# Moving a feed-forward's first norm into the output projection's loop, with half-token block products and first activations put ahead

## The chip, the cores and the metric

The kernel runs on one core of a Trainium2 chip. The metric is the device time of one execution in microseconds (us); of several runs the median is compared. TensorE multiplies matrices into PSUM, VectorE and ScalarE work element by element and can read PSUM, GpSimd works element by element in SBUF, and DMA transfers are issued from the queues of SyncE (loads) and ScalarE (stores).

## The reference, cut to what matters

Two layers run one after the other over 1024 tokens of width 1024. The first mixes tokens by windowed attention and a gated delta rule, projects the mix and applies a feed-forward. The change touches only this last part of the first layer:

```python
def _rmsnorm(x, w):
    ...
    y = x32 * lax.rsqrt(jnp.mean(x32 * x32, axis=-1, keepdims=True) + EPS)
    return (y * w.astype(jnp.float32)).astype(x.dtype)

def first_block(...):
    ...
        h = h + jnp.concatenate([attn, gdn], axis=-1) @ w_out[l]
        hn = _rmsnorm(h, norm_ffn_w[l])
        h = h + jnp.square(jax.nn.relu(hn @ w_ffn_in[l])) @ w_ffn_out[l]
    return _rmsnorm(h, norm_final_w)
```

w_out is 1024 x 1024, w_ffn_in 1024 x 4096 and w_ffn_out 4096 x 1024, all float32. The second layer follows and is not touched.

## The kernel before, in words

All large products are made in three matmuls each (`mm3`, `accumulate`): an operand is kept as a rounded part H and the rest L, and H·H, H·L and L·H are summed in PSUM. H is made by a cast on ScalarE; L by a subtraction on VectorE or GpSimd. `weight` (lines 103 to 113) loads a weight tile into one of three "raw" slots and splits it into one of eight "wh" and "wl" slots each.

The program says what is computed from what, in an order of text; the framework under it lays the tiles of the pools out in SBUF, orders the instructions of each engine by a plan made when the program is built, and makes a tile wait for the last use of what lay in its place before. So an engine's order need not be that of the text, but on the chip each engine and queue then keeps the order of the plan.

*Output projection.* First the attention half is projected, by column half n and token chunk i (128 tokens), into `Hs[i, n]`, 16 tiles of the pool "h" (lines 744 to 757). Then eight weight tiles are held in all the weight slots, and the loop of lines 762 to 787 goes over the eight chunks in the order 3, 4, 2, 5, 1, 6, 0, 7: ScalarE, GpSimd and VectorE prepare the gated and normed delta-rule output of the chunk (eight ScalarE operations), and TensorE multiplies it, 12 matmuls for each column half, which are added to `Hs` on VectorE (line 787).

*Norm of the feed-forward.* After the loop its pools and the PSUM pools are closed and new ones opened (lines 788 to 810). The loop of lines 829 to 861 goes over the chunks in the same order, p = 0 to 7: the sums of squares (line 164) and the root give a scale; `h` is stored to DRAM as the residual (line 835); VectorE scales (line 837); TensorE transposes eight blocks of 128 x 128 into two PSUM tiles (line 840). For the first four chunks ScalarE copies them as B00, B10, in float32 and as H, and VectorE makes L (lines 846, 826, 827). For the last four, VectorE forms the sums of a Strassen-like scheme against the first four, t1 to t4, and all are split into B11, T1, T2, T3, T4 (lines 851 to 861). A pair of such tiles takes 16 KB of each partition; the pool "xs" has 14 tiles of 8 KB, and "tx" six of 2 KB beside the norm's weights (4 KB).

*First product.* `strassen` (lines 904 to 933) makes 256 of the 4096 hidden rows in one of 16 groups: seven block products of 12 matmuls with 512 tokens each, where a plain product has eight. Two of them, A00 with B00 and A01 with B10, need only the first 512 tokens; the others need T2, T1, T3, T4 and B11, with weight sums S1 to S4 made on VectorE (lines 915, 916, 922, 930) from weights loaded to the pool "f1" (line 886; 44 KB, of which four weight tiles are 16, six sums 12, and eight tiles for results 16). Each group is a generator in two parts; lines 935 to 941 put the first part of group g + 2 behind the second part of group g. `hidden` (lines 897 to 902) adds, applies relu and square on VectorE, and stores to `hid_d` in DRAM.

*Second product.* Lines 963 to 983: for c = 0 to 7 four weight tiles of each column half are loaded and split, then 512 hidden rows are loaded (line 969) and split into D; at c = 0 the residual is loaded from `h_d` into the new tiles `Hs` (line 976); then 16 sums of 12 matmuls are added to `Hs` on VectorE (line 981).

Of the kernel before, what the change touches and what calls it, by code (L numbers as in the profile page):

```python
# [17 lines left out]
P = 128  # L18
# [38 lines left out]
def tile_hybrid_layers(ctx, tc, a, out):  # L57
# [464 lines left out]

    s2 = ctx.enter_context(ExitStack())
# [4 lines left out]
    op = pool(s2, "o", 8)  # L528
# [136 lines left out]

    project(*PA)
# [69 lines left out]
    s3.close()  # L736
    hpc = ctx.enter_context(ExitStack())
# [24 lines left out]
    for c in order:  # L762
# [20 lines left out]
        for n in range(2):  # L783
            ps = acc512()
            for k in range(4):
                mm3(ps, u, g[n][k], k == 0, k == 3, asl=hs(k))
            dve.tensor_add(Hs[c, n], Hs[c, n], ps)
    s4.close()
    s2.close()
# [8 lines left out]
    pm[0] = pool(pf, "pff", 6, space=PSUM)  # L798
    ptc = ctx.enter_context(ExitStack())
    pt = pool(ptc, "ptr", 2, space=PSUM)  # L800
    h_d, hid_d = scratch("h_d", [T, 1024]), scratch("hid_d", [4096, T])
# [4 lines left out]
    xsp = pool(s5, "xs", 14)  # L806
    txc = ctx.enter_context(ExitStack())
    txp = pool(txc, "tx", 6)
    wb = txp.tile([P, 1024], F32, name="wb", tag="wb", bufs=1)
    dma(wb, a["norm_ffn_w"][0].partition_broadcast(P))  # L810

    def xtile(name, dt=F32R):
        return xsp.tile([P, 4, 512], dt, name=name, tag="xs")

    def pair(name):
        return xtile(name + "h"), xtile(name + "l")

    def tx():
        return txp.tile([P, 4, P], F32, name="tx", tag="tx")


    B00f, B10f = xtile("x00", F32), xtile("x10", F32)
    B00, B10, B11, T2, T1, T3, T4 = (None,) * 7

    def halved(U, cs, src, eng):
        act.copy(U[0][:, :, cs], src)
        eng.tensor_sub(U[1][:, :, cs], src, f32(U[0][:, :, cs]))

    for p, i in enumerate(order):
        hv = [Hs[i, 0], Hs[i, 1]]  # L830
        cs = slice((p % 4) * P, (p % 4) * P + P)
        rs = rstd_of(hv)
        pq = []
        for j in range(2):
            put(h_d[i * P : (i + 1) * P, 512 * j : 512 * j + 512], hv[j])
            xs = tmp()
            dve.scalar_tensor_tensor(xs, hv[j], rs, wb[:, 512 * j : 512 * j + 512], op0=ALU.mult, op1=ALU.mult)
            ps = pt.tile([P, 512], F32, name="g", tag="g")
            for q in range(4):
                pe.transpose(ps[:, q * P : q * P + P], xs[:, q * P : q * P + P], ident)  # L840
            pq.append(ps.rearrange("p (k t) -> p k t", k=4))
        if p < 4:
            if p == 0:
                B00, B10 = pair("b00"), pair("b10")
            for U, Uf, src in ((B00, B00f, pq[0]), (B10, B10f, pq[1])):
                act.copy(Uf[:, :, cs], src)
                halved(U, cs, src, dve)
            continue
        if p == 4:
            B11, T2, T1, T3, T4 = (pair(n) for n in ("b11", "t2", "t1", "t3", "t4"))  # L850
        b11, t1, t2, t3, t4 = (tx() for _ in range(5))
        act.copy(b11, pq[1])
        dve.tensor_sub(t1, pq[0], B00f[:, :, cs])
        dve.tensor_sub(t3, b11, pq[0])
        halved(B11, cs, pq[1], dve)
        dve.tensor_sub(t2, b11, t1)
        halved(T2, cs, t2, gp)
        dve.tensor_sub(t4, B10f[:, :, cs], t2)
        halved(T1, cs, t1, dve)
        halved(T3, cs, t3, gp)  # L860
        halved(T4, cs, t4, dve)
    txc.close()
    hpc.close()

    f1 = ctx.enter_context(ExitStack())
# [543 lines left out]
```

## Time and profile before

| | |
|---|---|
| median of 3 runs | 2537.58 us (2537.42 to 2539.28) |
| the profiled execution's own time | 2540.82 us |
| its span, first to last instruction | 2538.7 us |
| mean granted TensorE clock | 0.971 |
| TensorE busy | 2353.8 us (93%), 10906 matmuls and transposes |
| VectorE, ScalarE, GpSimd busy | 1495.1, 1063.6, 982.7 us |
| moved by DMA | 310.43 MB |

Times in the rows count from the span's first instruction. A row of the timeline gives the start, the time taken, the engine, the line, the operation and its tiles; in square brackets stands the idle time of the engine before it and what ended it. Matmuls are pipelined, so the distance from start to start, not the time of one, says how fast they follow each other. PE is TensorE, DVE is VectorE, ACT ScalarE, POOL GpSimd and SP SyncE; a q behind the name is the engine's queue.

### The profile page before, as it was taken

How to read it: one execution, taken by the hardware profiler on the slowest of the kernel's cores; microseconds unless marked ns; L12 is line 12 of the kernel's file. 1: busy time of each engine (PE TensorE's matmuls, PEld its weight loads, DVE VectorE, ACT ScalarE, POOL GpSimd, SP SyncE). 2: the span in 40 equal slices, each digit the busy share in tenths (PEclk: the TensorE clock that was granted, in tenths of full speed). 3: DMA queues.
4: the chain of work that ended last, by engine and by line, in shares of the span. 5: the costliest groups of instructions: out<-in, count | busy, mean ns of one | idle time of the engine just before them, and what ended most of it. 6: DMA issues, size and time to landing. Idle time of an engine off the chain costs nothing. (4 is left out here: it accounts for less than half of the span.)

```text
span 2538.7 us, 31786 instructions
## 1 busy us (share of the span) xinstructions
PE 2353.8 (93%) x10906; PEld 1927.9 (76%) x10906; DVE 1495.1 (59%) x2726; ACT 1063.6 (42%) x2177; POOL 982.7 (39%) x822
## 2 busy tenths in 40 slices
PE   7898798989949999899999999989999999999998
PEld 5676578878738888788888788767777787888887
DVE  5779935776576555444344703989988885312113
ACT  5554214665542333222122522666555575233331
POOL 3346734433432122222223413445444443344353
PEclk9999999989969999999999999999999999999999
DMA  5785598655413333443232333222222225312123
GB/s 166 222 274 161 146 299 237 173 153 182 143 57 118 108 111 105 151 156 100 92 100 88 117 101 116 63 73 71 67 67 67 67 79 164 123 47 87 47 74 120
DMA packets 326228, 310.43 MB, mean 122 GB/s; under 512 B 46407, under 2 KB 243971, under 8 KB 326067
## 3 DMA queue, kind: packets, MB, share of 16 engines
q1 hardware_dynamic: 271827, 234.38, 31.5%
q10 hardware_dynamic: 54240, 74.03, 8.3%
q8 instruction: 86, 1.41, 0.2%
q14 instruction: 75, 0.61, 0.1%
HBM read 224.89 MB, written 85.54 MB: 122 GB/s over the span
## 5 line engine op out<-in xcount | busy, mean ns | idle before, releaser
L99 POOL TENSOR_TENSOR wl<-raw,wh 128x512 fp32r<-128x512 f32 x212 | 292.2, 1389 | 537.5 <-ACT wh L98 523.6
L147 PE MATMUL mm<-uh,wh 128*128 128x512 f32 x960 | 379.4, 395 | 0.2 <-DVE mx L1202 0.2
L149 PE MATMUL mm<-uh,wl 128*128 128x512 f32 x960 | 378.1, 394 | 0.0
L148 PE MATMUL mm<-ul,wh 128*128 128x512 f32 x960 | 377.7, 393 | 0.0
L98 ACT CAST wh<-raw 128x512 fp32r<-128x512 f32 (+1 forms) x213 | 129.4, 616 | 288.0 <-PE mm L149 105.7
L149 PEld LDWEIGHTS mm<-uh,wl 128*128 128x128 f32 x960 | 181.7, 189 | 39.5
L148 PEld LDWEIGHTS mm<-ul,wh 128*128 128x128 f32 x960 | 181.9, 189 | 35.5
L147 PEld LDWEIGHTS mm<-uh,wh 128*128 128x128 f32 x960 | 182.1, 190 | 34.9 <-DVE mx L1202 0.6
L147 PE MATMUL mm<-wh,hid 128*128 128x512 f32 x512 | 200.9, 393 | 8.0 <-ACT hid L98 8.0
L148 PE MATMUL mm<-wl,hid 128*128 128x512 f32 x512 | 200.3, 392 | 0.0
L149 PE MATMUL mm<-wh,hid 128*128 128x512 f32 x512 | 198.3, 389 | 0.0
L981 DVE TENSOR_TENSOR h<-h,mm 128x512 f32<-128x512 f32 x128 | 87.6, 686 | 174.1 <-PE mm L149 173.9
L147 PE MATMUL mm<-xnh,wh 128*128 128x512 f32 x352 | 145.5, 413 | 14.4 <-ACT t L300 6.6
L1151 POOL TENSOR_TENSOR ul<-u,uh 128x512 fp32r<-128x512 f32 (+3 forms) x96 | 105.6, 1101 | 134.7 <-DVE uh L1150 112.4
L110 POOL TENSOR_TENSOR wl<-raw,wh 128x512 fp32r<-128x512 f32 x72 | 101.9, 1415 | 121.2 <-DVE wh L109 46.5
L149 PE MATMUL mm<-xnh,wl 128*128 128x512 f32 x352 | 143.7, 408 | 0.0
L148 PE MATMUL mm<-xnl,wh 128*128 128x512 f32 x352 | 143.6, 408 | 0.0
L147 PEld LDWEIGHTS mm<-wh,hid 128*128 128x128 f32 x512 | 96.9, 189 | 28.8 <-ACT hid L98 8.4
L148 PEld LDWEIGHTS mm<-wl,hid 128*128 128x128 f32 x512 | 97.0, 189 | 20.1
L149 PEld LDWEIGHTS mm<-wh,hid 128*128 128x128 f32 x512 | 96.3, 188 | 20.0
L157 DVE TENSOR_SCALAR s<-s 128x512 f32<-128x512 f32 x32 | 26.3, 821 | 135.4 <-ACT s L156 135.4
L290 DVE SCALAR_TENSOR_TENSOR tc<-cv,cw,tc 128x512 f32<-128x512 f32 x96 | 98.2, 1023 | 4.8 <-ACT cv L278 2.9
(405 smaller groups left out, 5763.1 us busy)
## 6 DMA issues: line engine op xcount, KB each, us to landing
raw<-in_w_in SPq DMA_DIRECT2D x172, 256.0 KB
raw<-in_w_ffn_out SPq DMA_DIRECT2D x64, 256.0 KB
raw<-in_w_ffn_in SPq DMA_DIRECT2D x32, 512.0 KB
hid_d<-ht ACTq DMA_DIRECT2D x64, 256.0 KB
hr<-hid_d SPq DMA_DIRECT2D x32, 512.0 KB
e<-e_d SPq DMA_DIRECT2D x16, 512.0 KB
raw<-in_w_out SPq DMA_DIRECT2D x32, 256.0 KB
kv<-kv_d SPq DMA_DIRECT2D x16, 512.0 KB
```

What stands on the lines that cost most here:

```text
L98: act.copy(H, src)
L99: (eng or dve).tensor_sub(L, src, f32(H))
L110: gp.tensor_sub(L, raw, f32(H))
L147: pe.matmul(ps, A[0][:, asl], B[0][:, bsl], start=first, stop=False)
L148: pe.matmul(ps, A[0][:, asl], B[1][:, bsl], start=False, stop=False)
L149: pe.matmul(ps, A[1][:, asl], B[0][:, bsl], start=False, stop=last)
L157: dve.tensor_scalar(s, s, 1e18, 1.0, op0=ALU.min, op1=ALU.add)
L290: dve.scalar_tensor_tensor(acc, cv[:, o + t : o + t + 512], cw[:, t, c : c + 1], acc, op0=ALU.mult, op1=ALU.add)
L981: dve.tensor_add(Hs[order[p], n], Hs[order[p], n], ps)
L1151: gp.tensor_sub(uL[:, cs], u[:, cs], f32(uH[:, cs]))
```

## The change

The norm's work for a chunk becomes a function, `ffn_norm(p, banks)`, called inside the projection's loop two chunks late (for p - 2 after chunk p), for p = 6 behind the loop and for p = 7 between the first two of three half products. The tiles B00 and B10 lie in a new pool "xsa" opened before the loop; the transposed tiles of the last four chunks are copied to spare tiles of the pool "h" (`later`), and B11, T1, T2, T3 are built from them after the half products, in a pool "xsb"; T4 takes two tiles of "xsa" that are free by then. `half` makes a group's two products for the first 512 tokens; for the first three groups (`EARLY`) it is called ahead, with weights loaded through the "raw" slots. The generators are gone: each group follows whole. In the second product the hidden rows stand before the weights in the text, the first sums are copied into `Hs` on ScalarE, and the residual is loaded in quarters at c = 2 to 5 and added on GpSimd. The pool "o" is placed below those of the scan, which are closed earlier. The PSUM pool of the first product has eight tiles in place of six and two.

```diff
+    s2o = ctx.enter_context(ExitStack())
+    op = pool(s2o, "o", 8)
     s2 = ctx.enter_context(ExitStack())
...
-    op = pool(s2, "o", 8)
...
+
+    s2.close()
 
     project(*PA)
     project(*PZ)
...
     s3.close()
+    xac = ctx.enter_context(ExitStack())
+    xsa = pool(xac, "xsa", 6, side="right")
     hpc = ctx.enter_context(ExitStack())
     hp = pool(hpc, "h", 16, side="right")
...
 
     g = [[rows(WO, 4 + k, 512 * n) for k in range(4)] for n in range(2)]
     order = [3, 4, 2, 5, 1, 6, 0, 7]
-    for c in order:
+
+
+
+    h_d, hid_d = scratch("h_d", [T, 1024]), scratch("hid_d", [4096, T])
+    wb = xsa.tile([P, 1024], F32, name="wb", tag="wb", bufs=1)
+    dma(wb, a["norm_ffn_w"][0].partition_broadcast(P))
+
+    def xtile(name, dt=F32R, pl=xsa):
+        return pl.tile([P, 4, 512], dt, name=name, tag="xs")
+
+    def pair(name, pl=xsa):
+        return xtile(name + "h", F32R, pl), xtile(name + "l", F32R, pl)
+
+    def spare(name):
+
+        return hp.tile([P, 512], F32, name=name, tag="h")
+
+    def tx():
+        return spare("tx").rearrange("p (k t) -> p k t", k=4)
+
+    def halved(U, cs, src, eng):
+        act.copy(U[0][:, :, cs], src)
+        eng.tensor_sub(U[1][:, :, cs], src, f32(U[0][:, :, cs]))
+
+    B00f, B10f = xtile("x00", F32), xtile("x10", F32)
+    B00, B10 = pair("b00"), pair("b10")
+    later = {}
+
+    def ffn_norm(p, banks):
+        i = order[p]
+        hv = [Hs[i, 0], Hs[i, 1]]
+        cs = slice((p % 4) * P, (p % 4) * P + P)
+        rs = rstd_of(hv)
+        for j, ps in enumerate(banks):
+            put(h_d[i * P : (i + 1) * P, 512 * j : 512 * j + 512], hv[j])
+            xs = tmp()
+            dve.scalar_tensor_tensor(xs, hv[j], rs, wb[:, 512 * j : 512 * j + 512], op0=ALU.mult, op1=ALU.mult)
+            for q in range(4):
+                pe.transpose(ps[:, q * P : q * P + P], xs[:, q * P : q * P + P], ident)
+            src = ps.rearrange("p (k t) -> p k t", k=4)
+            if p < 4:
+                act.copy((B00f, B10f)[j][:, :, cs], src)
+                halved((B00, B10)[j], cs, src, dve)
+            else:
+                later[p, j] = tx()
+                act.copy(later[p, j], src)
+
+    for p, c in enumerate(order):
         o = OC[c]
         qT = gu.tile([P, 512], F32, name="l1", tag="l1")
         dma(qT.rearrange("p (h c) -> p h c", h=4), gq_d[:, :, c * P : (c + 1) * P].rearrange("h p c -> p h c"))
@@ -785,8 +837,11 @@
             for k in range(4):
                 mm3(ps, u, g[n][k], k == 0, k == 3, asl=hs(k))
             dve.tensor_add(Hs[c, n], Hs[c, n], ps)
+        if p > 1:
+            ffn_norm(p - 2, (bank(), bank2()))
+    ffn_norm(6, (bank(), bank2()))
     s4.close()
-    s2.close()
+    s2o.close()
     rb.close()
     pb.close()
     pmc.close()
...
     pf = ctx.enter_context(ExitStack())
-    pm[0] = pool(pf, "pff", 6, space=PSUM)
-    ptc = ctx.enter_context(ExitStack())
-    pt = pool(ptc, "ptr", 2, space=PSUM)
-    h_d, hid_d = scratch("h_d", [T, 1024]), scratch("hid_d", [4096, T])
+    pm[0] = pool(pf, "pff", 8, space=PSUM)
     x2_d = scratch("x2_d", [T, 1024])
     sv_d = scratch("sv_d", [T, 512])
     W2 = a["w_in_2"][0]
     s5 = ctx.enter_context(ExitStack())
-    xsp = pool(s5, "xs", 14)
...
-    for p, i in enumerate(order):
...
-    txc.close()
-    hpc.close()
-
-    f1 = ctx.enter_context(ExitStack())
-    fp = pool(f1, "f1", 4, side="right")
+    xsb = pool(s5, "xsb", 8)
...
+
+    first, EARLY = [], 3
+
+    def half(c0, A00, A01, mu, ht):
+
+        pa, pb_ = acc512(), acc512()
+        accumulate(pa, operand(A00, gp), B00, True)
+        m1 = mu("m1")
+        act.copy(m1, pa)
+        accumulate(pb_, operand(A01, gp), B10, True)
+        hidden(pb_, m1, c0, 0, ht)
+        return pa
+
+    def hidden(ps, other, row, h, ht):
+
+        t = ht("ht")
+        dve.tensor_add(t, other, ps)
+        dve.scalar_tensor_tensor(t, t, 0.0, t, op0=ALU.max, op1=ALU.mult)
+        put(hid_d[row : row + P, 512 * h : 512 * h + 512], t)
+
+    for g in range(EARLY):
+        A = []
+        for j in range(2):
+            raw = wp.tile([P, 512], F32, name="raw", tag="raw", bufs=3).rearrange("p (k m) -> p k m", k=4)
+            dma(raw, F1[512 * j : 512 * j + 512, 256 * g : 256 * g + P].rearrange("(k p) m -> p k m", p=P))
+            A.append(raw)
+        first.append(half(256 * g, *A, spare, spare))
+        if g == 0:
+            ffn_norm(7, (acc512(), acc512()))
+    B11, T2, T1, T3 = (pair(n, xsb) for n in ("b11", "t2", "t1", "t3"))
+    for p in range(4, 8):
+        cs = slice((p % 4) * P, (p % 4) * P + P)
+        b01, b11 = later[p, 0], later[p, 1]
+        t1, t2, t3 = (tx() for _ in range(3))
+        dve.tensor_sub(t1, b01, B00f[:, :, cs])
+        halved(B11, cs, b11, gp)
+        dve.tensor_sub(t2, b11, t1)
+        halved(T2, cs, t2, dve)
+        halved(T1, cs, t1, gp)
+        dve.tensor_sub(t3, b11, b01)
+        halved(T3, cs, t3, dve)
+        later[p] = tx()
+        dve.tensor_sub(later[p], B10f[:, :, cs], t2)
+    T4 = pair("t4")
+    for p in range(4, 8):
+        halved(T4, slice((p % 4) * P, (p % 4) * P + P), later[p], dve)
+    hpc.close()
+
+    f1 = ctx.enter_context(ExitStack())
+    fp = pool(f1, "f1", 4, side="right")
...
-    def strassen(c0):
-
+    def mu(name):
+        return fp.tile([P, 512], F32, name=name, tag="mu", bufs=4)
+
+    def ht(name):
+        return fp.tile([P, 512], F32, name=name, tag="ht", bufs=4)
+
+    def strassen(g):
+
+        c0 = 256 * g
         A00, A01, A10, A11 = blocks_of(F1, c0)
-        pa, pb_ = acc512(), acc512()
-        accumulate(pa, operand(A00, gp), B00, True)
-        m1 = mu()
-        act.copy(m1, pa)
-        accumulate(pb_, operand(A01, gp), B10, True)
-        hidden(pb_, m1, c0, 0)
-        yield
+        pa = first[g] if g < EARLY else half(c0, A00, A01, mu, ht)
         S1, S2, S3, S4 = (st() for _ in range(4))
         dve.tensor_add(S1, A10, A11)
         dve.tensor_sub(S2, S1, A00)
         accumulate(pa, operand(S2, dve), T2, False)
-        u2 = mu()
+        u2 = mu("u2")
...
+        u3 = mu("u3")
         act.copy(u3, pa)
-        hidden(pc, u3, c0 + P, 1)
+        hidden(pc, u3, c0 + P, 1, ht)
         pd = acc512()
         accumulate(pd, operand(A11, dve), T4, True)
...
-        hidden(pc, u2, c0, 1)
-        yield
-
-    runs = [strassen(256 * g) for g in range(16)]
-    next(runs[0])
-    next(runs[1])
+        hidden(pc, u2, c0, 1, ht)
+
     for g in range(16):
-        next(runs[g])
-        if g + 2 < 16:
-            next(runs[g + 2])
+        strassen(g)
     f1.close()
     s5.close()
-    ptc.close()
+    xac.close()
...
     Hs = {}
+    tiles = [(n, p) for n in range(2) for p in range(8)]
     for c in range(8):
         D = {}
-        g = [[rows(F2, 4 * c + k, 512 * n) for k in range(4)] for n in range(2)]
         for k in range(4):
             raw = hid.tile([P, 1024], F32, name="hr", tag="hr", bufs=3)
             dma(raw, hid_d[(4 * c + k) * P : (4 * c + k + 1) * P, :])
             for h in range(2):
                 D[k, h] = tuple(hid.tile([P, 512], F32R, name="hid", tag="hid") for _ in range(2))
                 split(*D[k, h], raw[:, 512 * h : 512 * h + 512])
-        if c == 0:
-            for n, p in [(n, p) for n in range(2) for p in range(8)]:
-                Hs[order[p], n] = hp.tile([P, 512], F32, name="h", tag="h")
-                dma(Hs[order[p], n], h_d[order[p] * P : (order[p] + 1) * P, 512 * n : 512 * n + 512])
-        for n, p in [(n, p) for n in range(2) for p in range(8)] if c < 7 else [(n, p) for p in range(8) for n in range(2)]:
+        g = [[rows(F2, 4 * c + k, 512 * n) for k in range(4)] for n in range(2)]
+        for n, p in tiles if c < 7 else [(n, p) for p in range(8) for n in range(2)]:
             ps = acc512()
             for k in range(4):
                 mm3(ps, D[k, p // 4], g[n][k], k == 0, k == 3, asl=hs(p % 4))
-            dve.tensor_add(Hs[order[p], n], Hs[order[p], n], ps)
+            if c == 0:
+                Hs[order[p], n] = hp.tile([P, 512], F32, name="h", tag="h")
+                act.copy(Hs[order[p], n], ps)
+            else:
+                dve.tensor_add(Hs[order[p], n], Hs[order[p], n], ps)
+
+        for n, p in tiles[4 * (c - 2) : 4 * (c - 1)] if 2 <= c < 6 else ():
+            r = tmp()
+            dma(r, h_d[order[p] * P : (order[p] + 1) * P, 512 * n : 512 * n + 512])
+            gp.tensor_add(Hs[order[p], n], Hs[order[p], n], r)
         if c == 6:
```

## Rows read from the trace of the kernel before

**Rows 1.** The page: busy time of an engine; granted clock in 40 slices, tenths

```profile
PE 2353.8 (93%) x10906; PEld 1927.9 (76%) x10906; DVE 1495.1 (59%) x2726; ACT 1063.6 (42%) x2177; POOL 982.7 (39%) x822
...
PEclk9999999989969999999999999999999999999999
```

**Rows 2.** By stretch: length; PE, PEld, DVE, ACT, POOL busy (count); clock, DMA, GB/s

```profile
660.00:705.00 45.00, 43.52 (x187) 33.76 (x185) 24.30 (x44) 24.41 (x55) 16.29 (x16) 1.00 0.37 126
704.92:753.51 48.59, 12.84 (x58) 9.81 (x57) 37.83 (x52) 21.92 (x41) 13.46 (x10) 0.56 0.09 28
753.51:1062.40 308.89, 307.75 (x1344) 253.41 (x1344) 180.69 (x254) 96.01 (x166) 75.28 (x55) 0.99 0.33 109
```

**Rows 3.** Timeline of TensorE around the projection's end

```profile
690.42 1.04 PE L840 MATMUL g<-ident,t 128*128 128x128 f32 x8
...
691.52 0.39 PE L148 MATMUL mm<-wl,guh 128*128 128x512 f32 x1
...
704.69 0.39 PE L149 MATMUL mm<-wh,gul 128*128 128x512 f32 x1
...
753.51 0.79 PE L878 MATMUL mm<-b00h,wh 128*128 128x512 f32 x1 [16.83 <-ACT wh L870]
...
758.44 0.41 PE L878 MATMUL mm<-b00l,wh 128*128 128x512 f32 x1
```

**Rows 4.** Groups of instructions, 650 to 760: busy us, mean ns | idle before

```profile
L837 DVE SCALAR_TENSOR_TENSOR t<-h,st,wb 128x512 f32<-128x512 f32 x16 | 13.8, 876 | 4.0 <-PE g L840 2.1 <-issue 1.3 <-POOL st L172 0.3
...
L164 ACT ACTIVATE junk<-h 128x512 f32<-128x512 f32 x16 | 10.0, 628 | 12.7 <-DVE h L787 12.5
...
L827 DVE TENSOR_TENSOR t1l<-tx,t1h 128x512 fp32r<-128x512 f32 x4 | 5.4, 1338 | 1.0 <-ACT t1h L826 1.0
...
L846 ACT COPY x<-g 128x512 f32<-128x512 f32 x8 | 4.7, 587 | 3.5 <-PE g L840 3.5
...
L827 DVE TENSOR_TENSOR b00l<-g,b00h 128x512 fp32r<-128x512 f32 x4 | 2.7, 687 | 0.0
```

**Rows 5.** Timeline of VectorE, then of the load queue, in the hole

```profile
720.40 0.68 DVE L853 TENSOR_TENSOR tx<-g,x 128x512 f32<-128x512 f32 x1
...
735.71 1.75 DVE L827 TENSOR_TENSOR t1l<-tx,t1h 128x512 fp32r<-128x512 f32 x1
...
745.29 3.58 DVE L827 TENSOR_TENSOR t4l<-tx,t4h 128x512 fp32r<-128x512 f32 x4
...
672.48 0.38 SPq L767 DMA_DIRECT2D l<-zs_d  x1
748.90 2.02 SPq L886 DMA_DIRECT2D raw<-in_w_ffn_in  x4
```

**Rows 6.** Groups of instructions of VectorE and ScalarE, 760 to 1062

```profile
L901 DVE SCALAR_TENSOR_TENSOR ht<-ht 128x512 f32<-128x512 f32 x63 | 56.8, 940 | 0.1
...
L915 DVE TENSOR_TENSOR sum<-raw,raw 128x512 f32<-128x512 f32 x15 | 11.5, 765 | 37.2 <-DMA raw<-in_w_ffn_in 37.2
...
L870 ACT CAST wh<-sum 128x512 fp32r<-128x512 f32 x61 | 37.9, 622 | 107.8 <-PE mm L878 86.4 <-DVE wl L871 20.9 <-DVE sum L930 0.4
```

**Rows 7.** Timeline of VectorE, start of the first product

```profile
754.38 0.97 DVE L915 TENSOR_TENSOR sum<-raw,raw 128x512 f32<-128x512 f32 x1 [5.51 <-issue]
...
767.52 0.68 DVE L900 TENSOR_TENSOR ht<-mu,mm 128x512 f32<-128x512 f32 x1
```

**Rows 8.** Timeline of TensorE, then of the load queue, second product's start

```profile
1062.17 0.39 PE L878 MATMUL mm<-b11h,wl 128*128 128x512 f32 x1
1070.59 0.79 PE L147 MATMUL mm<-wh,hid 128*128 128x512 f32 x1 [8.03 <-ACT hid L98]
...
1075.87 1.57 PE L149 MATMUL mm<-wh,hid 128*128 128x512 f32 x6
...
1045.17 19.62 SPq L106 DMA_DIRECT2D raw<-in_w_ffn_out  x8
1064.88 1.42 SPq L969 DMA_DIRECT2D hr<-hid_d  x3
```

More of the change, by code (lines that the diff above doesn't have):

```diff
@@ L805, in tile_hybrid_layers @@
     s5 = ctx.enter_context(ExitStack())
-    xsp = pool(s5, "xs", 14)
[L807 to L827, printed above, removed]
-    for p, i in enumerate(order):
[L830 to L861, printed above, removed]
-    txc.close()
-    hpc.close()
-    f1 = ctx.enter_context(ExitStack())
-    fp = pool(f1, "f1", 4, side="right")
+    xsb = pool(s5, "xsb", 8)
     def operand(src, eng):
@@ L892, in st @@
         return fp.tile([P, 4, P], F32, name="sum", tag="sum", bufs=6)
-    def mu():
-        return fp.tile([P, 512], F32, name="mu", tag="mu", bufs=4)
-    def hidden(ps, other, row, h):
-        t = fp.tile([P, 512], F32, name="ht", tag="ht", bufs=4)
-        dve.tensor_add(t, other, ps)
-        dve.scalar_tensor_tensor(t, t, 0.0, t, op0=ALU.max, op1=ALU.mult)
-        put(hid_d[row : row + P, 512 * h : 512 * h + 512], t)
-    def strassen(c0):
-        A00, A01, A10, A11 = blocks_of(F1, c0)
-        pa, pb_ = acc512(), acc512()
-        accumulate(pa, operand(A00, gp), B00, True)
-        m1 = mu()
-        act.copy(m1, pa)
-        accumulate(pb_, operand(A01, gp), B10, True)
-        hidden(pb_, m1, c0, 0)
-        yield
+    def mu(name):
[4 more added lines that the diff above has]
+        c0 = 256 * g
+        A00, A01, A10, A11 = blocks_of(F1, c0)
+        pa = first[g] if g < EARLY else half(c0, A00, A01, mu, ht)
         S1, S2, S3, S4 = (st() for _ in range(4))
@@ L923, in strassen @@
         accumulate(pa, operand(S3, gp), T3, False)
-        u3 = mu()
+        u3 = mu("u3")
         act.copy(u3, pa)
-        hidden(pc, u3, c0 + P, 1)
+        hidden(pc, u3, c0 + P, 1, ht)
         pd = acc512()
         accumulate(pd, operand(A11, dve), T4, True)
-        hidden(pd, u3, c0 + P, 0)
+        hidden(pd, u3, c0 + P, 0, ht)
         dve.tensor_sub(S4, A01, S2)
         accumulate(pc, operand(S4, dve), B11, False)
-        hidden(pc, u2, c0, 1)
-        yield
-    runs = [strassen(256 * g) for g in range(16)]
-    next(runs[0])
-    next(runs[1])
+        hidden(pc, u2, c0, 1, ht)
     for g in range(16):
-        next(runs[g])
-        if g + 2 < 16:
-            next(runs[g + 2])
+        strassen(g)
     f1.close()
     s5.close()
-    ptc.close()
+    xac.close()
     pf.close()
```

## The prediction

> **What bounds the kernel now.** I read the page first. TensorE is busy for 93% of the span, and the row of its granted clock is near full but for two dips [rows 1]; one of them, a 6 in the twelfth slice, is the place of the change. So a change pays where TensorE stands still or runs slowly, and hardly anywhere else. Next I read the busy times by stretch [rows 2]. In the output projection's loop TensorE is busy 43.5 of 45.0 us at full clock. In the next 48.6 us it has 58 instructions, nearly all transposes, at a granted clock of 0.56. Then the feed-forward's first product runs its 1344 matmuls in 308.9 us, and a last hole of 8 us follows at 1062 [rows 8]. The order of TensorE's instructions [rows 3] gives the edges. The projection's last matmul starts at 704.69, the feed-forward's first at 753.51. From 691.52 to 704.69 there are 58 steps, so one matmul of 512 columns takes 0.227 us.
>
> Who fills the hole is seen in the order of VectorE and of the load queue [rows 5]. From 720.40 until 745.29 + 3.58 = 748.87 VectorE builds the operands of tokens 512 to 1023, and the loads of the weights of the feed-forward are issued at 748.90, 0.03 us later. The queue stood empty from 672.48 until then. So these loads waited for memory that the building still used. Counted from the pool declarations, tiles of 112 KB (xs), 16 KB (tx and wb) and 32 KB (h) a partition were alive, and the 44 KB of the new pool had to lie on some of them.
>
> **The hole, removed.** The last matmul would be followed by another at 704.92. The first comes at 753.51, which is 48.6 us. The restart is slow as well: from 753.51 to 758.44 there are 10 steps [rows 3], 4.93 us where full speed needs 2.27, so 2.7 us more. Together 51.3 us stand there that TensorE need not spend.
>
> **Transposes, moved into TensorE's stream.** The hole held the transposes of seven chunks; the eighth set already ran in the loop. That set shows the price: 690.42 to 691.52 is 1.10 us for eight transposes and a matmul [rows 3], so 0.87 us for the eight. Seven sets are 6.1 us, now paid among matmuls. No matmul is added or removed.
>
> **Vector and Scalar work, moved into the loop.** ScalarE was busy 24.4 us between 660 and 705 [rows 2], 15 of the 16 squares included. It gains 16 copies for the first four chunks and about 5 for the next ones, at 0.587 us [rows 4]: 12.3 us. VectorE had 24.3 us; it gains 11 scalings (0.88) and 8 low parts (0.69) [rows 4], 15.2 us. Neither fills the loop, which grows to some 50 us. A norm comes two chunks (11 us) behind its sums, so its chain of squares, root and scaling is done when TensorE reaches the transposes. On TensorE the next chunk's matmuls are queued behind a transpose that waits. No row shows this for eight chunks. Bounds: 0, and 8 us (1 us for each chunk, about one scaling that is late). I take 1.0, as the one set in the loop waited for nothing.
>
> **Three half products as cover.** Each half is 24 matmuls, so three are 72 x 0.227 = 16.3 us; with the transposes of the last two chunks TensorE has 18.1 us of work after the loop. They need six loads of 256 KB into the three "raw" slots; the queue is empty then, and the cast of a load (0.62, [rows 6]) and its low part on GpSimd run beside the matmuls. The first cast needs a weight slot that the last chunk's first column half frees about 2.7 us before the loop's end, so I cost it at nothing. If that cover fails, one load is on the path: 748.90 to 753.51, 4.6 us.
>
> During these 18.1 us VectorE must finish B11, T2, T1 and T3 of four chunks. Before, 32 such operations and 7 scalings took 28.5 us [rows 5], 0.73 us each. Now T2 is complete after 21 operations of the build, 6 of the three halves' results, 2 scalings and an addition: 30, or 22 us after the loop if none of it comes earlier. Two of the chunks have their transposes in the loop, and then 18 remain, 13 us. So T2 comes 13 to 22 us after the loop against 18.1 us of cover: 0 to 4 us idle. Behind it come two sums and a cast, 2 x 0.77 + 0.62 = 2.2 us [rows 6], if their slots are freed only by the build. At the far end the weights' loads wait for the whole build again, as before: 28.5 + 4.6 + 1.5 - 18.1 = 16.5 us idle. By the pool declarations the new load tiles lie mostly on memory that is free by then, so I take 5.0 us, and a slow restart of 2.7 us: 7.7 (0 to 19.2).
>
> First stage: 51.3 - 6.1 - 1.0 - 7.7 = 36.5 us saved.
>
> A rule speaks against the last step. VectorE's operations with both inputs in SBUF took 1.34 us on average (T1's low parts), and 0.69 us where one input was in PSUM [rows 4]; single ones of the first kind, beside a GpSimd operation, took 1.75 [rows 5]. The Trainium skill (SBUF — State Buffer, section "SBUF: two separate sides") says that VectorE and GpSimd share a pair of ports, which one of them holds for a whole instruction while the other is fully blocked; the trace agrees in direction. What it would make of the sum is the second rival below.
>
> **The feed-forward's groups.** The hand-written lead of two groups is dropped. The order in the text is not the order on the engines: the first group's sum stands on VectorE at 754.38, its first result only at 767.52, though the text has them the other way round [rows 7]. So I expect sums still to be made early, and cost this at 0; the other end is the last rival.
>
> **The second product's start.** TensorE ends at 1062.17 + 0.23 and starts at 1070.59, 8.2 us later; the next 12 steps, to 1075.87, take 5.28 us in place of 2.72. That is 10.8 us [rows 8]. It waits for the hidden rows, whose loads are issued at 1064.88, behind eight weight loads that occupied the queue from 1045.17 on. The change puts the rows first in the text, and takes the 16 loads of the residual (4 MB) out of this place to four later groups, where TensorE never waits and the DMA engines are lightly used. The 16 additions go to GpSimd and are hidden there. The rows themselves were written long before. But their tiles can lie on the last result tiles of the first product. So 0 to 10.8; I take 8.0.
>
> **Sum.** 36.5 + 8.0 = 44.5 us. The profiled execution took 2540.82 us (span 2538.7 and 2.1 around it), so 2496.3 by its own time. It lay 3.2 us above the median of the runs, 2537.58; from that, 2493.1 us. About 0.2%, or 5 us, is what a measurement here can tell from no change. With idle and friction at nothing and all of 10.8, the saving is 51.3 - 6.1 + 10.8 = 56.0, so 2481.6; with the idle at 9 us and 6 us at the second start it is 51.3 - 6.1 - 1.0 - 11.7 + 6.0 = 38.5, so 2499.1. That is the forecast's own range, 2482 to 2499, with a chance of 0.56.
>
> **Rivals.** First, the late build: the sums' and weights' tiles wait for the whole build, 16.5 us idle. The first stage saves 36.5 - 11.5 = 25.0, all 33.0: 2504.6. For it speaks the 0.03 us between the last low part and the loads [rows 5]; against it the smaller demand on memory. 0.15.
>
> Second, VectorE and GpSimd in each other's way: the pace of 0.73 us already holds eight GpSimd low parts; the halves add six. If each lengthens one operation from 0.69 to 1.75, T2 comes 6.4 us later, which adds about 5 us of idle: 2498. It needs the last chunks' work to come wholly after the loop. 0.12. By the Trainium skill's rule (SBUF — State Buffer, the same section) this is the likely course.
>
> Third, the second start is not moved: 2493.1 + 8.0 = 2501. For it speaks that the rows' tiles may be released by the last writes of results only. 0.10.
>
> Fourth, ScalarE bounds the loop while it makes the copies: eight operations of preparation and two squares at 0.63 and four copies at 0.59 [rows 4] are 8.7 us a chunk, against 24 x 0.227 + 0.87 = 6.3 on TensorE. Over four chunks that is 9.6 us: 2502.7. Against it: ScalarE was busy 24.4 of 45 us there with all but the copies [rows 2]. 0.03.
>
> Fifth, slower: without the lead, each group's sums stand behind its first result on VectorE. Then TensorE waits in each of the 16 groups for L900, L901, two sums and a cast: 0.68 + 0.94 + 0.77 + 0.77 + 0.62 = 3.8 us [rows 6, 7], 61 us in all, and the time is 2493.1 + 61 = 2554. From 44.5/16 = 2.8 us a group on, the kernel is slower than before. Against it stands [rows 7]. 0.04.
>
> **Numbers.** The likeliest time is 2493. The forecast and the rivals but the last lie between 2482 and 2504.6; from 2481 to 2509, less than 2 in 10 is left out. Faster by over 0.2%: 0.94; the same, where half of the groups wait, 0.02; slower 0.04.
>
> **What would show it.** Right: in the changed kernel's trace transposes stand in eights between the projection's matmuls at full clock; matmuls of the halves follow within 1 us of the projection's last; the gap ahead of the first T2 product is under 9 us; the weights' loads come well ahead of it; the second product starts within 3 us of the first's end; and between those two the groups run at 0.227 us a matmul. Wrong: waits of TensorE on the sums in every group, a loop longer than 55 us from 654 on, or the loads issued behind the last low part of T4.

## The result, and the profile after

The changed kernel is slower: 2567.36 us median of four runs (2563.59 to 2574.41) against 2538.27 for the kernel before in the same batch, ratio 1.0118 (95% interval 1.0094 to 1.0141). The prediction said 2493. The profiled execution took 2563.59 us, its span was 2561.8, against 2540.82 and 2538.7 before.

The page of the changed kernel (it answers to [rows 1]):

```profile
PE 2362.0 (92%) x10906; PEld 1926.2 (75%) x10906; DVE 1481.0 (58%) x2710; ACT 1074.1 (42%) x2197; POOL 1010.6 (39%) x838
...
PEclk9999898999987999999999999999999999999999
```

The dip of the granted clock in the twelfth and thirteenth slice has not gone; it is now an 8 and a 7 shared between a slow loop and a hole. By stretch (columns as in [rows 2]):

```profile
650.00:700.00 50.00, 38.68 (x162) 29.77 (x160) 27.46 (x46) 27.69 (x59) 15.81 (x15) 0.90 0.29 95
700.00:745.00 45.00, 31.00 (x108) 23.27 (x109) 14.72 (x25) 20.95 (x43) 16.74 (x15) 0.77 0.20 64
745.00:765.00 20.00, 16.40 (x74) 12.54 (x72) 6.89 (x11) 4.10 (x7) 6.32 (x6) 1.00 0.40 131
765.00:790.00 25.00, 0.12 (x1) 0.12 (x1) 20.74 (x32) 9.86 (x18) 15.13 (x4) 0.54 0.23 74
```

From 650 to 745, where the loop runs, TensorE is busy 69.7 of 95 us and no other engine for much over half of the time; then come 20 us of half products, and 25 us with one TensorE instruction. What TensorE waited for between 640 and 1130 (us in total, times, longest):

```profile
PE mm L870 <- ACT wh L862: 26.7, 1, 26.7
PE mm L147 <- ACT guh L98: 14.0, 5, 3.4
PE g L805 <- DVE t L803: 10.1, 4, 2.9
PE mm L147 <- ACT hid L98: 8.0, 1, 8.0
```

The timeline of TensorE gives the edges (it answers to [rows 3] and [rows 8]). L828 is the matmul with ones in a chunk's preparation, L805 a norm's transpose:

```profile
623.26 1.02 PE L828 MATMUL g<-l,masks 128*128 128x512 f32 x2
...
664.87 0.60 PE L805 MATMUL g<-ident,t 128*128 128x128 f32 x4
665.31 1.02 PE L828 MATMUL g<-l,masks 128*128 128x512 f32 x2
...
743.13 0.47 PE L870 MATMUL mm<-b00h,wh 128*128 128x512 f32 x1 [0.87 <-DVE h L839]
...
789.88 0.79 PE L870 MATMUL mm<-t2h,wh 128*128 128x512 f32 x1 [26.72 <-ACT wh L862]
...
1095.92 0.79 PE L147 MATMUL mm<-wh,hid 128*128 128x512 f32 x1 [7.95 <-ACT hid L98]
```

The third pair with ones runs at 623.26, the fourth only at 665.31, right behind a norm's first transposes. Before, the eight pairs ran at 601, 615, 624, 638, 649, 660, 672 and 684, three to four chunks ahead of the projection's matmuls. The half products do follow the loop within 0.87 us, but the first T2 product comes 26.7 us after the last of them. VectorE and the load queue in that hole (they answer to [rows 5] and [rows 8]):

```profile
763.26 0.69 DVE L888 TENSOR_TENSOR ht<-m,mm 128x512 f32<-128x512 f32 x1 [4.19 <-PE mm L870]
763.86 0.68 DVE L906 TENSOR_TENSOR tx<-tx,x 128x512 f32<-128x512 f32 x1
...
782.86 0.68 DVE L789 TENSOR_TENSOR t4l<-tx,t4h 128x512 fp32r<-128x512 f32 x1
787.76 0.69 DVE L948 TENSOR_TENSOR sum<-raw,raw 128x512 f32<-128x512 f32 x1 [4.22 <-DMA raw<-in_w_ffn_in]
...
752.37 41.91 SPq L928 DMA_DIRECT2D raw<-in_w_ffn_in  x6
783.57 10.71 SPq L928 DMA_DIRECT2D raw<-in_w_ffn_in  x5
...
1090.15 1.43 SPq L996 DMA_DIRECT2D hr<-hid_d  x3
```

The build of T1 to T4 (L906 on) starts right behind the third half's result, 20.7 us after the halves began, and takes 19.7 us; then the first weight sum waits 4.2 us for its load. Of the queue's six loads from 752.37 on, five are issued only from 783.57 on, 0.03 us after the last low part of T4 has ended (782.86 + 0.68): they waited for memory that the build used. The rows of the second product are still loaded after the first product's end. So two of the prediction's own signs of being wrong are there, a loop longer than 55 us and loads behind the last low part of T4; the third, waits on the sums in every group, is not.

From the loop's first addition to the end of the first product, by the profiled executions:

| us | before | predicted | after |
|---|---|---|---|
| loop, first to last addition | 45.2 | 50.6 | 88.7 |
| from there to the end of the half products | | 18.1 | 20.9 |
| TensorE idle ahead of the first T2 product (before: from the loop to the first product) | 48.4 | 5.0 | 26.7 |
| the rest of the first product | 308.9 | 292.6 | 297.9 |
| sum | 402.5 | 366.3 | 434.2 |

The predicted loop is 45.2 + five sets of transposes of 0.87 + 1.0; the predicted rest is 308.9 - 16.3. The 67.9 us by which the sum missed, the 8.0 us that the second product's start did not give, less 6.3 us by which the loop began earlier and 2.3 us less for all that follows, are the 67.3 us between the 2496.3 forecast for the profiled execution and its 2563.59.

Of the loop's 88.7 us TensorE stood idle for some 25, where before it was 3. Most of the rest of the growth is slower work: at a granted clock of 0.90 and 0.77, where the loop before had 1.00 [rows 2], its matmuls took about 10 us more than at 0.227 us each, and the transposes came on top.

The prediction has no term for the stages ahead of the loop, and they are not the same. The change closes pools of the scan earlier and moves the pool "o", and between 350 and 400 us TensorE gets less done, first before, then after, with its longest wait there (from the waits between 260 and 660):

```profile
350.00:400.00 50.00, 46.44 (x257) 40.05 (x256) 14.22 (x43) 13.31 (x25) 19.18 (x18) 0.93 1.00 298
...
350.00:400.00 50.00, 40.43 (x194) 35.04 (x193) 12.46 (x40) 11.05 (x20) 20.44 (x22) 0.80 0.89 274
...
PE gi L574 <- issue: 8.0, 3, 6.4
```

Such a wait of 5.0 to 7.8 us at line 574, with the clock at 0.80 or 0.81, stands in the traces of all eleven kernels that have this part of the change, and in none of the three that do not (before, e3 and e4). Which line of the change brings it was not tested.

### The profile page after: what moved, and what is told of

Its sections match the earlier page's. It is cut to its first block, busy times and chain, and to the rows that moved or that the text cites. A ratio compares the mean times of both kernels' runs of the same rounds, so it can differ in the third digit from the quotient of the medians.

```text
span 2561.8 us, 31825 instructions
## 1 busy us (share of the span) xinstructions
PE 2362.0 (92%) x10906; PEld 1926.2 (75%) x10906; DVE 1481.0 (58%) x2710; ACT 1074.1 (42%) x2197; POOL 1010.6 (39%) x838
## 5 line engine op out<-in xcount | busy, mean ns | idle before, releaser
L1009 DVE TENSOR_TENSOR h<-h,mm 128x512 f32<-128x512 f32 x112 | 76.7, 685 | 154.2 <-PE mm L149 152.2
```

The costliest lines, as they stand in the source:

```text
L1009: dve.tensor_add(Hs[order[p], n], Hs[order[p], n], ps)
```

## The experiments

Twelve kernels, each beside the kernel before, whose medians in these batches were 2539.24 to 2541.64. Ratios are to the kernel before of the same batch, with 95% intervals. "Idle" is TensorE's wait ahead of the first T2 product, "start" its longest wait at the second product's start. Even with the same instructions the stages ahead differ from run to run: the loop's first addition came at 659.9, 662.6 and 656.9 us in the kernel before and in two variants that are equal to it up to there. So differences of 2 or 3 us are read from the stages. In the nine kernels below whose norm has a PSUM tag of its own, that addition came at 661.8 to 669.4 us: a part of what they gain in the loop seems to be lost ahead of it.

| kernel | loop | idle | start | median | ratio |
|---|---|---|---|---|---|
| changed | 88.7 | 26.7 | 8.0 | 2567.36 | 1.0118 (1.0094 to 1.0141) |
| e1_own_bank | 48.2 | 23.4 | 7.7 | 2534.44 | 0.9970 (0.9960 to 0.9981) |
| e2_more_l1 | 61.5 | 23.4 | 7.8 | 2539.26 | 0.9993 (0.9983 to 1.0004) |
| e3_second_only | 44.6 | | 8.3 | 2541.71 | 1.0002 (0.9992 to 1.0011) |
| e4_no_lead | 44.8 | | 7.8 | 2541.16 | 1.0004 (0.9994 to 1.0013) |
| e5_own_results | 48.3 | 19.9 | 7.7 | 2530.74 | 0.9955 (0.9938 to 0.9972) |
| e6_five_early | 48.3 | 27.2 | 7.9 | 2537.18 | 0.9984 (0.9973 to 0.9994) |
| e7_rows_memory | 48.6 | 24.6 | 3.4 | 2529.92 | 0.9951 (0.9934 to 0.9968) |
| e8_all_four | 49.2 | 17.6 | 3.4 | 2526.86 | 0.9944 (0.9926 to 0.9963) |
| e9_own_weights | 48.5 | 14.6 | 7.7 | 2528.40 | 0.9957 (0.9941 to 0.9973) |
| e10_joined | 48.6 | 4.5 | 3.2 | 2517.61 | 0.9915 (0.9895 to 0.9935) |
| e12_shifted | 48.1 | 24.5 | 3.4 | 2529.59 | 0.9954 (0.9940 to 0.9968) |
| e13_norm_spare | 50.4 | 9.2 | 3.4 | 2517.03 | 0.9909 (0.9895 to 0.9922) |

### The loop: e1 and e2

```diff
-            ffn_norm(p - 2, (bank(), bank2()))
+            ffn_norm(p - 2, (bank3(), bank2()))
...
-    ffn_norm(6, (bank(), bank2()))
+    ffn_norm(6, (bank3(), bank2()))
```

> The changed kernel, but the norm's first PSUM tile in the loop comes from a slot that nothing else uses there (bank3 in place of bank). Theory A (the loop grew because the norm's transposes and the preparation's matmul with ones share two PSUM slots, so that a preparation can no longer run ahead): the matmuls with ones stand again 3 or 4 chunks ahead, the loop from 653 to its last add takes 50 to 58 us in place of 89, and the kernel takes about 2530 us (2522 to 2540). Theory B (the loop grew because ScalarE takes squares and copies of the norm in order, ahead of the preparation's logarithm): the loop stays at 80 us or more and the time within 8 us of the changed kernel's 2567.

For e2 the changed kernel's four tiles of a preparation become eight:

```diff
-        qT = gu.tile([P, 512], F32, name="l1", tag="l1")
+        qT = gu.tile([P, 512], F32, name="l1", tag="l1", bufs=8)
```

and the same for `zt`, `zg` and `s`.

> The changed kernel, but with eight tiles in place of four for the preparation of a chunk (tag l1), so that two chunks can be prepared at once. Theory A (shared PSUM slots): the matmuls with ones still stand behind the transposes; loop 80 us or more, time within 8 us of 2567. Theory B (the preparations are one at a time because of their four tiles, and that alone sets the pace of 15 us a chunk): loop under 65 us, time about 2540.

Measured, by the additions to `Hs` and the matmuls with ones (ns min/median/max, first and last start in us), in e1:

```profile
L839 DVE TENSOR_TENSOR h<-h,mm x16: 674/680/689, 664.7 to 712.9; 128x512 f32<-128x512 f32 x16
...
L828 PE MATMUL g<-l,masks x16: 590/591/592, 609.4 to 690.5; 128*128 128x512 f32 x16
```

and in e2:

```profile
L839 DVE TENSOR_TENSOR h<-h,mm x16: 674/680/690, 659.8 to 721.3; 128x512 f32<-128x512 f32 x16
...
L828 PE MATMUL g<-l,masks x16: 590/592/1062, 609.9 to 704.9; 128*128 128x512 f32 x16
```

With a tag of its own for the norm the loop takes 48.2 us, 3.0 more than before, and the pairs with ones run 10 to 14 us apart with no hole. So the tag is what let the loop grow. In e2 the hole stays (624 to 671.5), and yet the loop takes only 61.5 us: here theory A's number was wrong and B's right. The two fit together. With the shared tag each later pair with ones stands in TensorE's order behind the transposes of the norm three chunks earlier, in the changed kernel as in e2. The lead of three or four chunks is gone, and each chunk goes through one chain alone: the pair with ones, logarithm and exponential on ScalarE, two products, the cast, the chunk's matmuls, a norm's transposes, and only then the next pair. With four tiles, for whose release the next chunk's loads wait, that is some 15 us a chunk (pairs at 665, 681, 696, 712 and 727). With eight, the last five pairs come at 672, 676, 683, 700 and 704. Theory A's wording was wrong in one thing: the fourth pair does not wait for a bank in use. It starts at 665.31, before ScalarE begins to read out the norm's transposes ahead of it (665.51), so it lies in the other of the two banks, and from that one the third pair's result had been read by 628.9. It waits for its turn in TensorE's order; that the order comes from the pool's giving out its tiles in the order of the text is argued from e1, not shown. ScalarE's order alone (theory B as applied to e1) is refuted.

### The second product's start and the lead: e3 and e4

e3 is the kernel before with the second product's part of the diff alone. e4 is the kernel before without the generators:

```diff
-    runs = [strassen(256 * g) for g in range(16)]
-    next(runs[0])
-    next(runs[1])
     for g in range(16):
-        next(runs[g])
-        if g + 2 < 16:
-            next(runs[g + 2])
+        for _ in strassen(256 * g):
+            pass
```

> The kernel before with the second product's part of the change alone (hidden rows ahead of the weights in the text, first sums copied to Hs, residual in quarters added on GpSimd). The prediction's step: 8 us less, 2530. Theory C (the rows' loads wait for memory of the first product and for the weights' loads whichever way the text goes): within 2 us of 2538, the first loads of hidden rows still issued about 2 us after the first product's last matmul. A cost of its own (16 copies on ScalarE, residual loads through the three temporary tiles) would show as 2540 to 2545.

> The kernel before with the generators dropped and each group of the first product written whole, nothing else. The prediction's step: no change (within 3 us of 2538). Rival five: 2.8 to 3.8 us more in each of 16 groups, 2583 to 2599. From the changed kernel's trace, where the first product's steady part took about 10 us more than its matmuls at full pace, a part of that, 0 to 10 us, is looked for here.

Both equal the kernel before. The load queue in e3:

```profile
1067.11 1.37 SPq L969 DMA_DIRECT2D hr<-hid_d  x3
```

The second product waits 8.3 us, and the rows' loads are issued 2.4 us after the first product's end (1064.67), where before it was 2.5: the order of the text moved nothing, and the residual's transfer, taken out of this place, had not been on the path. In e4 the lead was worth nothing.

### The hole behind the half products: e5, e6, e9

e5 is e1 and six tiles for the results of the halves, which had taken spare h tiles:

```diff
+    hf = pool(hfc, "hf", 3)
...
+    def early(name):
+        return hf.tile([P, 512], F32, name=name, tag=name)
...
-        first.append(half(256 * g, *A, spare, spare))
+        first.append(half(256 * g, *A, early, early))
```

> As e1_own_bank, and the results of the half products (m1, ht) lie in six tiles of their own, not in the spare h tiles from which the build of T1 to T4 takes its sums. Theory D (VectorE starts the build only at the third half's result because its tiles wait for the slots of the halves' results): the build starts about 724 in place of 734.9, the sums of the first group at about 744 in place of 754.5, TensorE's idle time ahead of the first T2 product falls from 23.4 to about 13 us, the time from 2534 to about 2524. Rival E (the build is late because of VectorE's order or because chunk 7's norm is late, whatever the slots): idle stays 21 to 24 us, time 2531 to 2537.

e6 is e1 with more cover:

```diff
-    first, EARLY = [], 3
+    first, EARLY = [], 5
```

> As e1_own_bank, with five half products ahead in place of three: 48 matmuls, 10.9 us, more cover behind the loop. If the idle time ahead of the first T2 product is a matter of too little cover, as the prediction's sum has it, it falls from 23.4 to about 12.5 us and the time to about 2524. Theory D: the build now waits for the fifth half's result in place of the third's, so it starts 10.9 us later; idle stays at 21 to 25 us and the time within 4 us of 2534.

VectorE in e5, and what two of its loads of weights waited for:

```profile
720.93 0.68 DVE L912 TENSOR_TENSOR tx<-tx,x 128x512 f32<-128x512 f32 x1
...
742.26 2.49 DVE L789 TENSOR_TENSOR t4l<-tx,t4h 128x512 fp32r<-128x512 f32 x4
749.15 0.69 DVE L955 TENSOR_TENSOR sum<-raw,raw 128x512 f32<-128x512 f32 x1 [4.40 <-DMA raw<-in_w_ffn_in]
...
SPq L935 <- DVE ht L888: 16.9, 1, 16.9
SPq L935 <- DVE t4l L789: 6.8, 1, 6.8
```

and in e6:

```profile
747.08 0.69 DVE L888 TENSOR_TENSOR ht<-m,mm 128x512 f32<-128x512 f32 x1 [4.19 <-PE mm L870]
747.68 0.68 DVE L906 TENSOR_TENSOR tx<-tx,x 128x512 f32<-128x512 f32 x1
```

With tiles of their own for the results, the build starts at 720.9 and not 734.9, and ends at 744.8. With five halves on the spare tiles it starts behind the fifth result, at 747.7, and 10.9 us more cover left 27.2 us idle where e1 has 23.4. So the build waited for slots that the halves' results held (theory D). The idle time in e5 fell less than expected, to 19.9 us. One of the two loads that the first sum needs waited for a result's tile until 737.55, the other for the last low part of T4 until 744.82, and the sum was 4.4 us late. e9 takes both away: the results go to the temporary tiles, and the weights get three tiles in memory that was free.

```diff
-            r = fp.tile([P, 4, 2 * P], F32, name="raw4", tag="raw4", bufs=4)
+            r = rp.tile([P, 4, 2 * P], F32, name="raw4", tag="raw4")
```

> As e5_own_results (norm's own bank, halves' results out of the spare tiles; here they take the three temporary tiles), and the first product's weight tiles are three of their own in the 12 KB that nothing else uses there, in place of four that overlap. Theory J (what is left of the idle time in e5, 19.9 us, is 4.4 us of waiting for the weights' loads, held up by memory, and for the rest the build itself): the loads land before the build ends, the first sum follows the last low part of T4 at once, idle 15 to 16 us, time about 4 us under e5's 2530.7. Rival K (three tiles are too few for the groups that follow): the first product's steady part gets longer by waits on weights, time 2531 or more.

```profile
751.09 2.48 DVE L789 TENSOR_TENSOR t4l<-tx,t4h 128x512 fp32r<-128x512 f32 x4
753.49 0.68 DVE L952 TENSOR_TENSOR sum<-raw,raw 128x512 f32<-128x512 f32 x1
```

The first sum follows the last low part of T4 at once, idle 14.6 us: theory J. The time did not follow: the ratio equals e5's. From the first half product to the first T2 product it is 35.1 us against 37.8, since TensorE now waits 2.1 us at the last norm, whose scalings share the temporary tiles; what else was lost lies ahead of the loop (its first addition came at 668.6, in e5 at 661.8) and stays open.

### The rows' memory: e7

e1, with the tiles of the hidden rows on B00's place.

```diff
+    hrp = pool(hpc, "hr", 3, side="right")
     hp = pool(hpc, "h2", 16, side="right")
...
-            raw = hid.tile([P, 1024], F32, name="hr", tag="hr", bufs=3)
+            raw = hrp.tile([P, 1024], F32, name="hr", tag="hr")
```

> As e1_own_bank, but the tiles of hidden rows (hr) lie where B00 was, free since the last group's first half, and not on the first product's weight tiles. Theory F (the rows' loads stand behind the weights' loads in the queue because their memory comes free late, and those wait for the first product's end): three row loads are issued some 8 us or more ahead of the first product's end, the second product starts within 3 us of it in place of 7.7, time 2526 to 2530. Rival G (what is late is something else, the splitting of the rows into tiles that lie on the first product's results, or the rows' own storing): gap 6 us or more, time 2532 to 2537.

The load queue, then ScalarE:

```profile
1043.03 1.44 SPq L997 DMA_DIRECT2D hr<-hid_d  x3
1044.93 14.45 SPq L106 DMA_DIRECT2D raw<-in_w_ffn_out  x5
...
1059.98 1.14 ACT L98 CAST hid<-hr 128x512 fp32r<-128x512 f32 x2 [2.29 <-DVE ht L889]
```

The loads go out 14 us ahead of the first product's end (1057.1), in front of the weights' loads in which they had been stuck. The wait fell from 7.7 to 3.4 us. What is left is, by the trace, ScalarE's order: the cast of the rows stands behind the store of the last result, which waits for VectorE. Theory F, with 3.4 us where under 3 was expected.

### A pace: e12

In the changed kernel's trace the matmuls of one group do not all follow each other alike:

```profile
900.02 0.39 PE L870 MATMUL mm<-t2h,wh 128*128 128x512 f32 x1
...
902.51 0.39 PE L870 MATMUL mm<-t2h,wl 128*128 128x512 f32 x1
902.74 0.39 PE L870 MATMUL mm<-t4h,wl 128*128 128x512 f32 x1
...
907.87 0.39 PE L870 MATMUL mm<-b10h,wh 128*128 128x512 f32 x1
```

From 900.02 to 902.51 are 11 steps, 0.226 us each, with T2 as the streamed operand; from 902.74 to 907.87 are 22 steps of 0.233 with T4 and B00. e12 is e7 with 448 bytes of padding.

```diff
+    padp = pool(xac, "pad", 1, side="right")
+    dve.memset(padp.tile([P, 112], F32, name="pad", tag="pad"), 0.0)
     xsa = pool(xac, "xsa", 6, side="right")
```

> As e7_rows_memory, with 448 bytes of padding under the pool xsa, so that B00, B10 and T4 start 32 bytes past a multiple of 128, as B11, T1, T2 and T3 do, and not 96. In the changed kernel's trace matmuls that stream B00, B10 or T4 follow each other at 0.233 us and those that stream the others at 0.227; in the kernel before all do at 0.227. Theory H (where the operand's rows start decides the pace): all at 0.227, the first product shorter by 36 x 16 x 0.0066 = 3.8 us, time about 3.8 us under e7's 2529.9. Rival I (the upper part of the memory, or what shares it, is slower): still 0.233, same time.

The same in e12:

```profile
899.64 0.39 PE L872 MATMUL mm<-t1h,wl 128*128 128x512 f32 x1
...
901.90 0.39 PE L872 MATMUL mm<-t4h,wh 128*128 128x512 f32 x1
...
903.26 0.39 PE L872 MATMUL mm<-t2h,wh 128*128 128x512 f32 x1
```

Ten steps of T1 take 2.26 us and six of T4 1.36: 0.226 and 0.227. From the first to the last T2 product it is 284.5 us, against 288.1 in e7: 3.6 us, theory H. The medians don't resolve it (0.9954 against 0.9951), but the traces agree: the steps with B00, B10 and T4 take 0.233 us on average in all eight kernels that have the pool xsa without the padding, and 0.227 in the three with it (e10, e12, e13) and in the three without the pool (before, e3, e4).

### Together: e8, e10, e13

e8 is e1, e5, five halves and e7. e10 is e9, five halves, e7 and e12. e13 is e10 with

```diff
-            xs = tmp()
+            xs = tmp() if p < 7 else spare("t")
```

> The norm's own bank, own tiles for the halves' results, five half products ahead, and the rows' tiles on B00's place, together. By theories A, D and F the gains add up: idle ahead of the first T2 product about 2 us, second start within 3 us, time 2534 - 21 - 6 = about 2507 (2502 to 2514). If any of the gains only moves a wait to another place, 2515 or more.

> e9 with five half products ahead, the rows' tiles on B00's place (e7), and the tiles of the pool xsa shifted by 448 bytes (e12). Expected if the parts add up: idle ahead of the first T2 product 5 to 10 us (15.5 less 10.9 of cover, and 2 to 4 us more of build, since VectorE is slower beside the low parts that GpSimd makes for two more halves), second start within 4 us, steady part 3.8 us shorter: 2507 to 2514. If a gain moves a wait, 2520 or more.

> As e10_joined, but the scaled tokens of the last chunk's norm take two spare h tiles and no temporary ones. In e10 TensorE waited 5.5 us for that norm's two scalings (730.95 to 733.36), which stood behind the first half's result because both want the three temporary tiles. If the tiles are what holds it, the first scaling stands ahead of that result, most of the 5.5 us goes, and the time falls by 3 to 5 us, to 2513 to 2515 (ratio to the kernel before about 0.990). If the build of T1 to T4 on VectorE sets the end anyway, the idle time moves to the first T2 product and the time stays at 2516 to 2519.

e8 missed by 20 us: the weights' loads were issued at 754.68, when the last half's tiles had been read, and the first sum waited for them:

```profile
761.21 0.69 DVE L955 TENSOR_TENSOR sum<-raw,raw 128x512 f32<-128x512 f32 x1 [5.83 <-DMA raw<-in_w_ffn_in]
```

That led to e9. e10 missed its 2507 to 2514 by some 4 us: its idle time is even a little under the forecast (4.5 us), but it lost 5.5 us at the last norm:

```profile
PE mm L807 <- DVE t L805: 5.5, 2, 3.8
PE mm L873 <- ACT wh L865: 4.5, 1, 4.5
```

In e13 that wait shrinks and the other grows:

```profile
PE mm L873 <- ACT wh L865: 9.2, 1, 9.2
...
PE mm L807 <- DVE t L805: 2.3, 1, 2.3
```

The time stays (2517.03), as its expectation has it for the case that the build sets the end, and VectorE works without a gap from the first half's result (726.49) to the first sums (757.63). So the end of the build on VectorE, not the tiles, sets this stage now; the scaling still stands behind that result (727.09). e10 and e13 beat both kernels: 2517.0 us is 24.6 under the kernel before of its batch and some 50 under the changed one.

## Why the prediction was wrong

**The step that failed first** is the loop's friction: "I take 1.0, as the one set in the loop waited for nothing", with 8 us as the far bound. The loop grew by 43.5 us where 5.4 was forecast. What the step looked at, TensorE's queue behind a late transpose and the busy time of VectorE and ScalarE, was right: in e1 the loop grew by 3.0 us with all of that in it (in the changed kernel TensorE waited 10.1 us for the norm's scalings, in e1 1.7). What it left out is the PSUM tag. `bank()` serves the preparation's matmul with ones and, by the diff, the norm too. The one set that "waited for nothing" in the kernel before took its tiles from another pool. e1 shows the cause, e2 how it acts. The Trainium skill (Perfetto Trace Analysis, section "Optimization Strategy") says that the same gap coming again and again on the engine that should be full can mean too little SBUF or PSUM for the next tile; the trace agrees: 14.0 us in five waits for `guh`, none over 3.4, and 5.1 us in two with more tiles (e2).

**The residual idle time**, 5.0 us forecast, 26.7 measured, is the second. The step's length for the build was about right (13 to 22 us for T2; it took 16.7, the whole build 19.7), but it let the build start with the loop's end. It started with the third half's result, since the halves' results and the build's sums share the spare tiles (e5, e6). That the length fitted is in part luck: its pace of 0.73 us comes from 32 operations and 7 scalings in 28.5 us, and the trace of the kernel before has 28 and 3 there, 0.92 us each; after the change VectorE ran at 0.68. The first rival, the late build, had the other piece right, weights that wait for memory until the build ends (4.2 us; e8, e9), and was too small at 16.5, as it too took the cover as running beside the build.

**The second product's start**: 8.0 us forecast, nothing measured, the third rival. The step's own warning, that the rows' tiles can lie on the first product's, was the cause, by way of the queue: late memory put the loads behind weights' loads that wait for slots (e3, e7).

**Right were**: the transposes' price and the loop without the shared tag (e1); the halves that follow within 1 us; the generators at nothing (e4), and so against the fifth rival; the slow restart, 4.70 us from 789.88 to 794.58 for 11 steps, 2.2 more than at full speed. ScalarE did not bound the loop (27.7 of 50 us busy), the fourth rival.

**The second rival**, VectorE and GpSimd in each other's way: in the changed kernel's build two operations of VectorE took 1.75 us, beside GpSimd's low parts, and the others 0.68, so it cost VectorE about 2 us; in e5 four operations of the build, from 722 to 734, took 1.75 to 1.79. GpSimd lost more:

```profile
774.04 10.62 POOL L789 TENSOR_TENSOR t1l<-tx,t1h 128x512 fp32r<-128x512 f32 x1 [3.69 <-ACT t1h L788]
```

This low part of T1, where the other three of GpSimd's in this build took 1.25 to 1.71 us, ended 1.1 us after VectorE's unbroken run of the build. This agrees with the Trainium skill (SBUF — State Buffer, section "SBUF: two separate sides"), where such an operation of VectorE and one of GpSimd exclude each other, but it was not what set the time.

**Not foreseen**: the slower pace of the operands in the new pool, 3.6 us (e12); the loss in the stage from 350 to 400 us, which the prediction put at nothing without a word; and the lower clock in the loop. What the second costs by the loop's start stays open, since that start moves by some 6 us between runs of kernels that are equal up to there.

## What to carry to other kernels

When work is moved into a loop, list every pool and tag that it takes tiles from and who else takes from it there: an engine's free time says nothing when the pool gives its tiles out in turn, and a lead of several iterations is lost first. Cover hides a chain only if the chain can start beside it, so ask which tiles the covering work holds; e6 added 10.9 us of cover and idled longer. And a load that is put earlier in the text goes no earlier while its tiles lie on memory in use.

## What the runs showed of the hardware

Matmuls of 128 x 512 in float32 that streamed B00, B10 or T4 followed each other at 0.233 us in the eight kernels with the pool xsa as the change places it, and at 0.227 in the three where 448 bytes of padding shift it (e10, e12, e13). In the built program, whose places no trace holds, these tiles start 96 bytes past a multiple of 128 in their partition without the padding and 32 with it, as the tiles with 0.227 do. Only these two offsets were tried.

A GpSimd subtraction that reads SBUF took 10.62 us beside a run of VectorE operations with both inputs in SBUF, where the other three of its kind took 1.25 to 1.71 us; VectorE's own took 1.75 beside such a subtraction and 0.68 otherwise.
